# A one-core hybrid block: the second half of q turned by VectorE over DRAM, x1's tiles transposed eight at a time, and another slab order

## The chip, the core and the metric

One core of a Trainium2 chip runs the whole kernel in one launch. The metric is the device time of one execution in microseconds. PE is the matrix engine (TensorE), DVE VectorE, ACT ScalarE, POOL GpSimd, SP the engine whose queue issues most of the DMAs. Each engine runs its own list of instructions in the order in which the program gives them; an instruction that waits holds up all that stand behind it on its engine.

## What is computed

One layer of a trunk with two branches, 512 rows of 1024 columns, float32:

```python
h = rms_norm(x, norm_pre)
(aq, ak, av, az, dq, dk, dv, db, da, dz, gate_att, gate_dn) = split_cols(h @ w_in)
q, k = apply_rope(rms_norm(heads(aq))), apply_rope(rms_norm(heads(ak)))       # 8 and 2 heads of 128
y_att = (gqa_attention(q, k, heads(av)) * silu(az)) @ w_br_att
qkv = silu(short_conv(concatenate([dq, dk, dv])))
o_dn = bidir_gated_deltanet(l2_norm(cq) * 128 ** -0.5, l2_norm(ck), cv, g, beta)   # chunks of 64, both ways
y_dn = (rms_norm(o_dn, dn_norm) * silu(dz)) @ w_br_dn
mix = (sigmoid(gate_att) * y_att + sigmoid(gate_dn) * y_dn) @ w_out
x = x + rms_norm(mix, norm_post)
x = x + rms_norm(sigmoid(x @ w_ple_gate) * (p @ w_ple_proj), ple_norm)
```

The products must hold float32 accuracy, which the kernel reaches by splitting both operands of a gemm into a rounded high half and the rest as a low half, and adding three products: low weight by high data, high by low, high by high.

## The kernel before

**Slabs.** All large weights come in slabs of 128x1024 float32. ACT casts a slab to its high half (`whi`), and POOL (L102) or DVE (L97) subtracts that from the slab to get the low half (`wlo`). A slab with the 512 rows of h takes 24 matmuls of 128x512: L553 to L555 in `gemm_t` for slabs as the stationary operand (dq, dk, dv, az, dz, gA, gB, ydn), L590 to L592 and L572 to L574 where the data is stationary (kv, q0, q1, out0, out1, pg0, pg1). The yatt slabs have their own lines, L1861 for low-by-high and high-by-high, L1845 for high-by-low.

**What sets the order.** The program is laid out by a planner (`Flow`) before anything runs. Its parts are generators; each has a priority, and each step of a part gets an estimated time on its engine. The gemms form one stream of the lowest priority (10), which runs the slab jobs in the order of the table `ORDER`. All other work (convolutions, the chunked recurrence, the heads of attention, the tails of each gemm) are parts with priorities from the table `PR`, and the planner puts their instructions between the matmuls of the stream when it believes their operands ready. So the slab order decides which matmuls PE has at hand while a chain of small steps runs on the other engines. `COOL` and `HOT` are the thresholds by which `split` gives the low half of a slab to POOL or DVE; `EXPS` decides whether an exponential of the recurrence is eight small ACT activations (L983) or one DVE addition (L987) and one large ACT activation; `EOUT` delays a few writes; `VGAP` spaces the steps of the recurrence's preparation.

**The halves of q.** q is computed in two halves of four heads, q0 and q1, each with a tail for every 128 rows (`q_tail`, L1514 on): row norms, rotary turn, then the transpose that the scores need. For a half listed in `QTURN` the tile goes through `small_blocks` (one DVE transpose of 32x32 blocks), is written to a DRAM tensor `Bq` and read back by four DMAs into a tile `c` in the order that completes the transpose (`turned`), and `landed` casts it on ACT and subtracts on POOL or DVE. A half that isn't listed is transposed by four PE matmuls with the identity into a bank `aux` (L1541), and ACT and DVE take the two halves from that bank.

**Attention and its neighbours.** `att_heads` (L1632) runs the scores of a group of four heads: three matmuls (L1657 to L1659) for each head and 128 rows, DVE's maximum of the row, a small scaling on POOL (`sm`), the exponential on ACT, a 32x32 transpose on DVE. Then come the weighted sums, 192 matmuls at L1734, which need each head's tile split into high (ACT) and low (DVE, L97, `blk`). `yatt_two` begins the first two yatt slabs with the half of the rows that the first group of heads gave and finishes them when the second group is done. The inverse of the chunk matrices ends at L1152 and L1167 on PE, with two DVE scalings (64x512) behind, and the recurrence begins at L1222.

**The end.** out0 and out1 give the two halves of x1's row tiles. `out1_tail` normalises and adds; of the four row tiles the first (`TURNED = 1`) goes over DRAM as above, the others are transposed by PE in two groups of four, one for each half, into one `aux` bank each (L1969). pg0 and pg1 follow.

Of the kernel before, what the change touches and what calls it, by code (L numbers as in the profile page):

```python
# [35 lines left out]
class Flow:  # L36
# [87 lines left out]
    def run(self):  # L124
        while self.parts:
# [32 lines left out]


ORDER = """  # L160
dq1 dk2 dk1 dk0 dq3 dk3 dq0 dq2 dv2 az4 dq6 az3 dk5 dv3 dq4 gB6
gA2 dk4 az7 dz1 dz4 dv1 gB5 dz2 az6 dv0 gB0 dq5 dq7 dk6 gB4 dk7
gA0 az0 gB3 dz6 dv6 dv7 gA6 gA5 dv4 dz0 az2 kv dv5 gB2 vec gA7
gB1 az1 dz3 az5 gA3 dz5 q0 dz7 gA1 q1 gA4 gB7 free_h ydn1 ydn2 ydn6
ydn3 ydn0 ydn5 ydn7 ydn4 yatt7 yatt4 yatt6 heads_on0 yatt3 yatt5 yatt0 yatt2 yatt1 heads_on1 out0
out1 pg0 pg1
"""
OUT0 = 'yatt3 yatt1 yatt2 yatt4'
PR = dict(dec=5, dm1=2, y=7, conv=1, gate=6, kv=4, q=9, head=7, ple=9, prep=1, tab=9)
GAP = 0.0  # L170
EXPS = 0.11
SP13 = 480.0
SPARE = ((15, "raw", 7.0, 190.0), (11, "pair", 22.0, 80.0), (12, "pair", 22.0, 80.0), (14, "pair", 279.0, 375.0),
         (13, "pair", 443.0, SP13), (6, "pair", 560.0, 640.0), (14, "raw", 590.0, 640.0))
EOUT = 27.01
WIDE = 2.0
LAND = "c2"
QTURN = (0,)
TURNED = 1
YTURN = ()  # L180
LONG, NEAR = 0.6, 1.5
X_DVE = ()
WARM = 5.5
PVB = 0.695
VGAP = 1.5
HEADHOT = 1
BATCH, TURN = 4, 0.3
SPAREMM = 2
W1 = 0
COOL, HOT = 10.41, -0.29  # L190


@with_exitstack
def layer(ctx, tc, x, xT, pw0, wp1, wt, wba, wn, rows, qkn, hd16, npost, pnorm, dnorm, cs, out):
    nc = tc.nc
    pe, act, dve, pool, sync = nc.tensor, nc.scalar, nc.vector, nc.gpsimd, nc.sync
# [40 lines left out]
    def unit(i, shape, dt=F32):  # L237
        return tile(f"u{i}", shape, dt)

    def bank(tag, shape=(128, 512)):  # L240
        cnt[0] += 1
        return ps.tile(list(shape), F32, tag=tag, bufs=caps[tag], name=f"{tag}_{cnt[0]}")
# [214 lines left out]


    slab, blocks, fetched = {}, {}, {}
    taken, weighed = Event(), Event()  # L460

    lent = {"raw": {}, "pair": {}}
    held = {}
# [1 line left out]
    def lend(u, kind, t0, t1):  # L465

        yield "at", t0
        yield "get", f"u{u}"
        w = unit(u, [128, 2, 1024], F32 if kind == "raw" else F32R)
        tags = [f"{kind}{u}_{i}" for i in range(2 if kind == "raw" else 1)]  # L470
        for i, tag in enumerate(tags):
            F.slots[tag] = [F.now]
            lent[kind][tag] = w[:, i] if kind == "raw" else w
        yield "at", t1
        for tag in tags:
            del lent[kind][tag]
        for tag in tags:
            yield "get", tag
        free(f"u{u}")
# [1152 lines left out]
    def att_heads(g):  # L1632
# [60 lines left out]

        yield "get", "u14"
        ring = unit(14, [128, 2, 2, 16, 32], F32R)
        for i in range(2):
            F.slots[f"ring{i}"] = [F.now]

# [237 lines left out]
    def out1_tail(t, o, need):  # L1936
# [10 lines left out]
        for half, src in enumerate((late["mx0"][:, t, :], o)):  # L1947
# [5 lines left out]
            if t < TURNED:  # L1953
                yield "at", tr - 0.5
                yield "get", "f2"
                T, te = small_blocks(xa[:, hs], tr)
                yield "at", te - 0.5
                yield "get", LAND
                L = tile(LAND, [128, 4, 4, 32])
                tw, te = turned(T, te, f"Bx{t}{half}", L)  # L1960
                free("f2", tw)
                ends.append((L, te))
                continue
            yield "at", tr + 0.3
            yield "get", "aux"
            pt = bank("aux", [128, 4, 128])
            for j in range(4):
                k = half * 4 + j
                pe.transpose(pt[:, j, :], xa[:, k * 128:(k + 1) * 128], ident)  # L1969
            yield "pe", 0.436  # L1970
            cc = slice(t * 128, (t + 1) * 128)
            _, te = split(pt, x1Th[half][:, :, cc], x1Tl[half][:, :, cc], F.now, 512)
            free("aux", te)
        for half, (L, te) in enumerate(ends):
            yield "at", te - 0.5
            te = landed(L, te, x1Th[half], x1Tl[half], t)
        return te + 0.2

    def out_job(half, us):
# [269 lines left out]
```

## Time and profile before

| | |
|---|---|
| three runs | 734.19, 735.26, 736.13 us (median 735.26) |
| the profiled execution | 732.72 us, its span 731.0 us |
| first weight-stationary matmul of the program's own work (L1370) | 5.85 us after the span's start |
| last PE matmul's end | 723.9 us |
| DMA | 121.64 MB, mean 166 GB/s |

The busy figures, the chain, PE's waits and the windows stand in the prediction. To read them: a timeline row is the start in us, the duration in us, the engine, the line, the operation, out<-in by the program's names, the shape, the number of instructions joined in the row, and in brackets the engine's idle time before it with what ended it. Matmuls overlap, so a matmul's duration is longer than the time from its start to the next one's start; the latter is what PE spends on it. Every helper that records an operation has one line (L122 for most, L97 and L102 for the two subtractions), so rows are told apart by names and shapes.

### The profile page before, as it was taken

How to read it: one execution, taken by the hardware profiler on the slowest of the kernel's cores; microseconds unless marked ns; L12 is line 12 of the kernel's file. 1: busy time of each engine (PE TensorE's matmuls, PEld its weight loads, DVE VectorE, ACT ScalarE, POOL GpSimd, SP SyncE). 2: the span in 40 equal slices, each digit the busy share in tenths (PEclk: the TensorE clock that was granted, in tenths of full speed). 3: DMA queues.
4: the chain of work that ended last, by engine and by line, in shares of the span. 5: the costliest groups of instructions: out<-in, count | busy, mean ns of one | idle time of the engine just before them, and what ended most of it. 6: DMA issues, size and time to landing. Idle time of an engine off the chain costs nothing.

```text
span 731.0 us, 12273 instructions
## 1 busy us (share of the span) xinstructions
PE 718.7 (98%) x4577; PEld 601.3 (82%) x4577; DVE 496.2 (68%) x914; ACT 352.6 (48%) x669; POOL 307.4 (42%) x293
## 2 busy tenths in 40 slices
PE   9999999999999999999999999999999999999996
PEld 7688888888789898888888888888888778888885
DVE  4688979889785667896946443658979974314534
ACT  6658653753651365435442236345746554323522
POOL 5836495111421265114411145655344638163501
PEclk9999999999999999999999999999999999999999
DMA  9854529856421324767350234695468568337313
GB/s 355 301 175 133 195 87 282 265 173 230 103 96 37 101 101 113 234 202 201 121 158 15 87 115 142 198 226 155 163 196 207 192 220 309 135 95 256 110 57 117
DMA packets 79051, 121.64 MB, mean 166 GB/s; under 512 B 24400, under 2 KB 42768, under 8 KB 78992
## 3 DMA queue, kind: packets, MB, share of 16 engines
q1 hardware_dynamic: 78848, 120.73, 52.4%
q8 instruction: 36, 0.59, 0.3%
q14 instruction: 23, 0.19, 0.1%
q10 hardware_dynamic: 144, 0.13, 0.1%
HBM read 94.98 MB, written 25.85 MB: 165 GB/s over the span
## 4 chain that ended last, share of the span: by engine, by line
PE 85%; DVE 8%; ACT 3%; issue 2%; DMA 1%; POOL 1%; POOLq 0%; SPq 0%; DVEq 0%; ACTq 0%
PE mm L553 15%; PE mm L555 14%; PE mm L554 14%; PE mm L574 4%; PE mm L572 4%; PE mm L573 4%; PE mm L592 3%; PE mm L590 3%; PE mm L591 3%; DVE f L122 3%; PE aux L1222 2%; PE aux L1254 2%; PE aux L1240 2%; PE aux L1213 1%; PE aux L1202 1%
## 5 line engine op out<-in xcount | busy, mean ns | idle before, releaser
L553 PE MATMUL mm<-u,wlo 128*128 128x512 f32 x488 | 195.9, 402 | 0.4 <-DVE wlo L97 0.4
L555 PE MATMUL mm<-u,whi 128*128 128x512 f32 x488 | 190.4, 390 | 0.0
L554 PE MATMUL mm<-u,whi 128*128 128x512 f32 x488 | 190.2, 390 | 0.0
L102 POOL TENSOR_TENSOR wlo<-wraw,whi 128x1024 fp32r<-128x1024 f32 x47 | 113.0, 2406 | 178.4 <-ACT whi L122 146.9
L553 PEld LDWEIGHTS mm<-u,wlo 128*128 128x128 f32 x488 | 91.8, 188 | 19.7 <-ACT u L122 0.8
L555 PEld LDWEIGHTS mm<-u,whi 128*128 128x128 f32 x488 | 91.6, 188 | 19.7
L554 PEld LDWEIGHTS mm<-u,whi 128*128 128x128 f32 x488 | 91.8, 188 | 17.0
L122 ACT CAST whi<-wraw 128x1024 fp32r<-128x1024 f32 x61 | 63.9, 1047 | 57.6 <-PE mm L555 20.1
L122 DVE SCALAR_TENSOR_TENSOR f<-mm,cw,f 128x510 f32<-128x510 f32 (+1 forms) x96 | 71.4, 746 | 9.0 <-ACT f L122 6.6
L102 POOL TENSOR_TENSOR u<-wraw,u 128x1024 fp32r<-128x1024 f32 x18 | 43.1, 2403 | 27.6 <-ACT u L122 26.0
L572 PE MATMUL mm<-u,u 128*128 128x512 f32 (+1 forms) x136 | 51.8, 381 | 0.0
L574 PE MATMUL mm<-u,u 128*128 128x512 f32 (+1 forms) x136 | 51.3, 377 | 0.0
L573 PE MATMUL mm<-u,u 128*128 128x512 f32 (+1 forms) x136 | 51.2, 377 | 0.0
L122 DVE TENSOR_TENSOR u<-aux,u 128x512 f32<-128x512 f32 (+2 forms) x49 | 31.6, 664 | 12.9 <-PE aux L1043 6.4
L122 ACT COPY c<-aux 128x512 f32<-128x512 f32 x18 | 10.4, 585 | 48.2 <-DVE f L122 35.4
L590 PE MATMUL mm<-whi,u 128*128 128x512 f32 x80 | 31.4, 393 | 0.0
L122 ACT ACTIVATE mm<-f 128x512 f32<-128x512 f32 x24 | 14.4, 600 | 35.0 <-DVE f L122 35.0
L592 PE MATMUL mm<-whi,u 128*128 128x512 f32 x80 | 31.2, 390 | 0.0
L591 PE MATMUL mm<-wlo,u 128*128 128x512 f32 x80 | 31.1, 389 | 0.0
L102 POOL TENSOR_TENSOR u<-u,u 128x1024 fp32r<-128x1024 f32 (+1 forms) x11 | 22.0, 2004 | 20.9 <-ACT u L122 15.6
L574 PEld LDWEIGHTS mm<-u,u 128*128 128x128 f32 x136 | 25.6, 188 | 4.8
L573 PEld LDWEIGHTS mm<-u,u 128*128 128x128 f32 x136 | 25.6, 188 | 4.6
(297 smaller groups left out, 1504.2 us busy)
## 6 DMA issues: line engine op xcount, KB each, us to landing
wraw<-in_wt_dram SPq DMA_DIRECT2D x58, 512.0 KB, 3.6
wraw<-in_wn_dram SPq DMA_DIRECT2D x24, 512.0 KB, 4.1
u<-in_wt_dram SPq DMA_DIRECT2D x14, 512.0 KB, 6.3
u<-CI SPq DMA_DIRECT2D x16, 256.0 KB, 5.5
u<-VD SPq DMA_DIRECT2D x16, 256.0 KB, 6.7
u<-in_x_dram SPq DMA_DIRECT2D x4, 512.0 KB, 7.6
u<-in_xT_dram SPq DMA_DIRECT2D x4, 512.0 KB, 8.2
eD<-u SPq DMA_DIRECT2D x8, 256.0 KB, 9.0
```

Of the source, the lines that this page charges most:

```text
L102: ins = fn(*a, **k)
L122: fn(*a, **k)
L553: pe.matmul(o, lo[:, k, :], mh(k), start=(k == 0), stop=False)
L554: pe.matmul(o, hi[:, k, :], ml(k), start=False, stop=False)
L555: pe.matmul(o, hi[:, k, :], mh(k), start=False, stop=(k == 7))
L572: pe.matmul(o, b, hi, start=(i == 0), stop=False)
L573: pe.matmul(o, a, lo, start=False, stop=False)
L574: pe.matmul(o, a, hi, start=False, stop=(i == 7))
L590: pe.matmul(o[t], b, hi, start=(k == 0), stop=False)
L591: pe.matmul(o[t], a, lo, start=False, stop=False)
L592: pe.matmul(o[t], a, hi, start=False, stop=(k == 7))
L1222: pe.matmul(pw[:, h, :], Vm[g][d][:, 4 * c + h, :], r[:, h, :], start=True, stop=True)
```

## The change

`ORDER` and `OUT0` are new permutations of the same slabs; PR, EXPS, EOUT, VGAP, COOL and HOT get other values; QTURN lists both halves of q; `out1_tail` takes two banks and transposes both halves of a tile in one run; and `lend` of unit 14, which lends its space to a slab, now waits for an event that `att_heads` sets once the ring of the second group has that unit.

```diff
-OUT0 = 'yatt3 yatt1 yatt2 yatt4'
-PR = dict(dec=5, dm1=2, y=7, conv=1, gate=6, kv=4, q=9, head=7, ple=9, prep=1, tab=9)
+OUT0 = 'yatt5 yatt1 yatt7 yatt0'
+PR = dict(dec=0, dm1=11, y=5, conv=1, gate=4, kv=2, q=7, head=8, ple=3, prep=7, tab=9)
-EXPS = 0.11
+EXPS = 0.94
-EOUT = 27.01
+EOUT = 37.16
-QTURN = (0,)
+QTURN = (0,1)
-VGAP = 1.5
+VGAP = 1.2
-COOL, HOT = 10.41, -0.29
+COOL, HOT = 8.39, -3.14
...
+        if u == 14 and t0 > 500.0:
+            yield "ev", ringed
...
         ring = unit(14, [128, 2, 2, 16, 32], F32R)
+        if g == 1:
+            ringed.set(F.now)
...
-            yield "at", tr + 0.3
+        for half, (L, te) in enumerate(ends):
+            yield "at", te - 0.5
+            te = landed(L, te, x1Th[half], x1Tl[half], t)
+        if t < TURNED:
+            return te + 0.2
+        yield "at", tr + 0.3
+        pts = []
+        for half in range(2):
             yield "get", "aux"
-            pt = bank("aux", [128, 4, 128])
+            pts.append(bank("aux", [128, 4, 128]))
+        for half, pt in enumerate(pts):
             for j in range(4):
                 k = half * 4 + j
                 pe.transpose(pt[:, j, :], xa[:, k * 128:(k + 1) * 128], ident)
-            yield "pe", 0.436
-            cc = slice(t * 128, (t + 1) * 128)
+        yield "pe", 0.872
+        cc = slice(t * 128, (t + 1) * 128)
+        for half, pt in enumerate(pts):
             _, te = split(pt, x1Th[half][:, :, cc], x1Tl[half][:, :, cc], F.now, 512)
             free("aux", te)
```

Of the table of slabs only the part around attention is shown, first the two lines before and then the two after:

```diff
-gB1 az1 dz3 az5 gA3 dz5 q0 dz7 gA1 q1 gA4 gB7 free_h ydn1 ydn2 ydn6
-ydn3 ydn0 ydn5 ydn7 ydn4 yatt7 yatt4 yatt6 heads_on0 yatt3 yatt5 yatt0 yatt2 yatt1 heads_on1 out0
+gA5 gA7 gA1 gB7 dz2 q0 az5 dz5 q1 gB5 gB4 free_h ydn0 ydn3 ydn7 ydn4
+ydn6 ydn5 ydn2 heads_on1 ydn1 yatt6 yatt0 yatt2 yatt7 yatt5 yatt1 yatt4 yatt3 heads_on0 vec out0
```

The program's order on the engines follows from this, with the line numbers of the later places moved by 2 to 9 (L553 is L555 after, L1657 is L1659, L1734 is L1738, L1861 is L1865). The first place is on PE, before the change, at the end of the q1 stage: the third group of q1's transposes, the end of the slab gB7 (`mm_4948`) and the first scores.

```order
L555 MATMUL mm_4948<-u_14_137,whi_4848 128x512
L1541 MATMUL aux_4997<-ident,f_661_4915 128x128 x4
L553 MATMUL mm_4948<-u_14_137,wlo_4849 128x512
L554 MATMUL mm_4948<-u_14_137,whi_4848 128x512
L555 MATMUL mm_4948<-u_14_137,whi_4848 128x512
L1657 MATMUL mm_5013<-u_417_3249,u_580_4394 128x512
```

After the change PE passes there from the last slab of h (gB4, `mm_4972`) to the scores with no transpose between.

```order
L555 MATMUL mm_4972<-u_14_137,wlo_4907 128x512
L556 MATMUL mm_4972<-u_14_137,whi_4906 128x512
L557 MATMUL mm_4972<-u_14_137,whi_4906 128x512
L1659 MATMUL mm_5030<-u_410_3232,u_576_4406 128x512
L1660 MATMUL mm_5030<-u_410_3232,u_575_4405 128x512
```

All four L1541 rows (of four transposes each) are gone; what they wrote now comes through the tiles `c` below. The second place is on POOL, in the score stage of the first group of heads, before the change: the small scalings `sm` of the softmax and low halves of slabs, and behind them the products with the gate.

```order
L102 TENSOR_TENSOR wlo_5009<-wraw_4901,whi_5008 128x1024
L122 TENSOR_SCALAR sm<-sm,saq 128x1 x11
L102 TENSOR_TENSOR wlo_5141<-wraw_5022,whi_5140 128x1024
L122 TENSOR_SCALAR sm<-sm,saq 128x1 x5
L102 TENSOR_TENSOR wlo_5232<-wraw_5058,whi_5231 128x1024
L102 TENSOR_TENSOR u_716_5264<-u_716_5264,gi_5359 128x512
```

After the change the same stretch of POOL, where the tiles `c` are those that the reads of Bq fill for q1:

```order
L122 TENSOR_SCALAR sm<-sm,saq 128x1 x5
L102 TENSOR_TENSOR u_621_4702<-c_669_5014,u_620_4701 128x4x128
L122 TENSOR_SCALAR sm<-sm,saq 128x1 x3
L102 TENSOR_TENSOR u_621_4702<-c_672_5024,u_620_4701 128x4x128
L122 TENSOR_SCALAR sm<-sm,saq 128x1
L102 TENSOR_TENSOR wlo_5153<-wraw_5037,whi_5152 128x1024
L122 TENSOR_SCALAR sm<-sm,saq 128x1 x3
L102 TENSOR_TENSOR u_621_4702<-c_679_5038,u_620_4701 128x4x128
L102 TENSOR_TENSOR wlo_5232<-wraw_5080,whi_5231 128x1024
L122 TENSOR_SCALAR sm<-sm,saq 128x1 x4
```

Three of q1's four subtractions have moved in between the scalings (the fourth is on DVE), each behind its cast on ACT. The third place is on PE, from the last score to the first weighted sums of the second group, before the change; the rows left out are those of ydn7 (`mm_5804`), ydn4 (`mm_5872`) and the first yatt slab (`mm_5928`).

```order
L1659 MATMUL aux_5811<-u_417_3249,u_625_4692 128x512
L553 MATMUL mm_5804<-u_354_2801,wlo_5680 128x512
...
L555 MATMUL mm_5872<-u_575_4389,whi_5801 128x512
L1861 MATMUL mm_5928<-u_753_5590,wlo_5864 128x512
L1861 MATMUL mm_5928<-u_753_5590,whi_5863 128x512
...
L1845 MATMUL mm_5928<-u_754_5591,whi_5863 128x512 x4
L1734 MATMUL aux_5857<-blk_5887,u_752_5589 128x512
```

After the change, with three matmuls of ydn2 (`mm_5797`), ydn1 (`mm_5922`) and the first yatt slab (`mm_5972`):

```order
L1661 MATMUL mm_5880<-u_410_3232,u_620_4701 128x512
L555 MATMUL mm_5797<-u_571_4401,wlo_5673 128x512
...
L555 MATMUL mm_5922<-u_350_2820,wlo_5772 128x512
L557 MATMUL mm_5922<-u_571_4401,whi_5771 128x512
L1865 MATMUL mm_5972<-u_754_5652,wlo_5893 128x512
L1865 MATMUL mm_5972<-u_754_5652,whi_5892 128x512
...
L1738 MATMUL aux_5911<-blk_5916,u_753_5651 128x512
```

Between the last score and the first yatt matmul stand 45 rows before and 27 after; 12 yatt matmuls stand ahead of the weighted sums before and 6 after, and the six others have moved behind the sums. The last score, of three matmuls, now stands directly behind two others of its head.

More of the change, by code (lines that the diff above doesn't have):

```diff
@@ L160 @@
 ORDER = """
-dq1 dk2 dk1 dk0 dq3 dk3 dq0 dq2 dv2 az4 dq6 az3 dk5 dv3 dq4 gB6
-gA2 dk4 az7 dz1 dz4 dv1 gB5 dz2 az6 dv0 gB0 dq5 dq7 dk6 gB4 dk7
-gA0 az0 gB3 dz6 dv6 dv7 gA6 gA5 dv4 dz0 az2 kv dv5 gB2 vec gA7
-gB1 az1 dz3 az5 gA3 dz5 q0 dz7 gA1 q1 gA4 gB7 free_h ydn1 ydn2 ydn6
-ydn3 ydn0 ydn5 ydn7 ydn4 yatt7 yatt4 yatt6 heads_on0 yatt3 yatt5 yatt0 yatt2 yatt1 heads_on1 out0
+dq0 dk2 dk1 dk3 dq1 dk0 dq3 dq2 dv2 dz4 dk5 az4 dq4 dv3 dq7 dz6
+gB0 dk4 dz3 gB1 az1 dv1 az3 gA0 gA4 dv0 az6 dq6 dk7 az2 dz1 dq5
+dk6 gB3 gB6 gA2 dv7 gA6 dv4 dz7 gA3 gB2 kv dv6 az0 dv5 dz0 az7
+gA5 gA7 gA1 gB7 dz2 q0 az5 dz5 q1 gB5 gB4 free_h ydn0 ydn3 ydn7 ydn4
+ydn6 ydn5 ydn2 heads_on1 ydn1 yatt6 yatt0 yatt2 yatt7 yatt5 yatt1 yatt4 yatt3 heads_on0 vec out0
 out1 pg0 pg1
 """
-OUT0 = 'yatt3 yatt1 yatt2 yatt4'
-PR = dict(dec=5, dm1=2, y=7, conv=1, gate=6, kv=4, q=9, head=7, ple=9, prep=1, tab=9)
+OUT0 = 'yatt5 yatt1 yatt7 yatt0'
+PR = dict(dec=0, dm1=11, y=5, conv=1, gate=4, kv=2, q=7, head=8, ple=3, prep=7, tab=9)
 GAP = 0.0
-EXPS = 0.11
+EXPS = 0.94
 SP13 = 480.0
@@ L459, in layer @@
     slab, blocks, fetched = {}, {}, {}
-    taken, weighed = Event(), Event()
+    taken, weighed, ringed = Event(), Event(), Event()
     lent = {"raw": {}, "pair": {}}
@@ L1962, in out1_tail @@
                 ends.append((L, te))
-                continue
-            yield "at", tr + 0.3
+        for half, (L, te) in enumerate(ends):
[6 more added lines that the diff above has]
+        for half in range(2):
             yield "get", "aux"
-            pt = bank("aux", [128, 4, 128])
+            pts.append(bank("aux", [128, 4, 128]))
+        for half, pt in enumerate(pts):
             for j in range(4):
@@ L1969, in out1_tail @@
                 pe.transpose(pt[:, j, :], xa[:, k * 128:(k + 1) * 128], ident)
-            yield "pe", 0.436
-            cc = slice(t * 128, (t + 1) * 128)
+        yield "pe", 0.872
+        cc = slice(t * 128, (t + 1) * 128)
+        for half, pt in enumerate(pts):
             _, te = split(pt, x1Th[half][:, :, cc], x1Tl[half][:, :, cc], F.now, 512)
             free("aux", te)
-        for half, (L, te) in enumerate(ends):
-            yield "at", te - 0.5
-            te = landed(L, te, x1Th[half], x1Tl[half], t)
         return te + 0.2
```

## The prediction

> **What bounds the kernel now.** I read the page's busy line and its chain first.
>
> ```profile
> PE 718.7 (98%) x4577; PEld 601.3 (82%) x4577; DVE 496.2 (68%) x914; ACT 352.6 (48%) x669; POOL 307.4 (42%) x293
> PEclk9999999999999999999999999999999999999999
> PE 85%; DVE 8%; ACT 3%; issue 2%; DMA 1%; POOL 1%; POOLq 0%; SPq 0%; DVEq 0%; ACTq 0%
> ```
>
> PE is busy 98% of the span, at nine tenths or more of its clock in every slice, and carries 85% of the chain that ended last. So the time is PE's work plus the few places where it stands still. Those places are listed by the waits of PE.
>
> ```profile
> PE mm L2110 <- POOL ident masks.py:199: 1.4, 1, 1.4
> PE mm L1861 <- DVE u L97: 0.7, 1, 0.7
> PE aux L1132 <- issue: 0.7, 1, 0.7
> PE mm L1861 <- POOL wlo L102: 0.6, 1, 0.6
> PE mm L675 <- POOL u L102: 0.4, 1, 0.4
> PE mm L553 <- DVE wlo L97: 0.4, 1, 0.4
> PE mm L881 <- DVE partk L122: 0.3, 1, 0.3
> PE aux L1486 <- DVE f L97: 0.3, 1, 0.3
> PE mm L1370 <- DVE u L97: 0.2, 1, 0.2
> ```
>
> Behind the first row, which belongs to the start, only eight waits stand, 3.6 us in all. A new order can gain no more than that by better hiding; everything else must come from work taken off PE. It can lose far more, since every one of the slab jobs needs its low half in time. The engine nearest to PE is DVE, and the windows show where it is fullest.
>
> ```profile
> 500.00:520.00 20.00, 20.00 (x90) 16.48 (x90) 17.36 (x31) 11.68 (x28) 8.41 (x16) 1.00 0.30 93
> 520.00:540.00 20.00, 20.00 (x207) 16.49 (x206) 18.39 (x31) 14.03 (x27) 6.32 (x5) 1.00 0.64 213
> 560.00:580.00 20.00, 19.35 (x84) 15.34 (x83) 17.98 (x30) 12.65 (x27) 10.22 (x12) 1.00 0.78 253
> 580.00:600.00 20.00, 19.30 (x227) 15.61 (x226) 15.93 (x22) 11.75 (x17) 6.63 (x4) 1.00 0.46 165
> ```
>
> After the length the columns are PE, PEld, DVE, ACT, POOL. Through the scores and the first weighted sums of attention (500 to 540) PE has no gap although DVE is busy 17.4 and 18.4 of 20 us; at 560 to 600 PE loses 0.65 and 0.70. This is the stage into which the change puts new DVE and POOL work.
>
> **The change part by part.**
>
> *Transposes of q1.* The four groups of L1541 go. What one costs PE is seen between its neighbours:
>
> ```profile
> 494.79 0.39 PE L555 MATMUL mm<-u,whi 128*128 128x512 f32 x1
> 495.02 0.60 PE L1541 MATMUL aux<-ident,f 128*128 128x128 f32 x4
> 495.37 0.47 PE L553 MATMUL mm<-u,wlo 128*128 128x512 f32 x1
> 495.69 0.39 PE L554 MATMUL mm<-u,whi 128*128 128x512 f32 x1
> 495.91 0.39 PE L555 MATMUL mm<-u,whi 128*128 128x512 f32 x1
> ```
>
> A 128x512 matmul follows its predecessor by 0.23 us. From the group's start to the next matmul are 0.35, and that one holds the next for 0.32, 0.09 more than usual: 0.44 for a group, four groups **-1.77 us**. All of it is PE time in a stage without PE gaps, so it is gained unless PE waits for it later. [...]
>
> In its place, per tile: one DVE block transpose, one write and four reads over DRAM, an ACT cast and a POOL or DVE subtraction instead of the same pair from the bank.
>
> ```profile
> L1541 PE MATMUL aux<-ident,f 128*128 128x128 f32 x16 | 2.4, 272 | 0.0
> L122 DVE STREAM_TRANSPOSE f<-f 128x512 f32<-128x512 f32 x12 | 8.3, 702 | 0.1
> L102 POOL TENSOR_TENSOR u<-c,u 128x512 fp32r<-128x512 f32 x4 | 5.2, 1292 | 0.0
> L97 DVE TENSOR_TENSOR u<-c,u 128x512 fp32r<-128x512 f32 x6 | 4.4, 734 | 10.8 <-ACT u L122 10.7
>   ACT u L122: 7.8, 4
> ```
>
> DVE pays 4 x 0.70 and is spared three subtractions of about 0.73, since the order puts three of the four on POOL at 1.29: +0.6 us on DVE, +3.9 on POOL, both off PE's path as long as the scores keep their distance. The last row is from the view of the tile Bq, the waits that it caused, here of half q0: its four casts on ACT waited 7.8 us together for the reads, nearly 2 us each. Behind such a cast on ACT now stand softmax exponentials and slab casts, and behind the POOL subtraction the small scalings that the exponentials need. Half q0 paid this in a stage of plain gemms and PE did not feel it. On SP the 20 new DMAs stand between slab loads. I cost it at nothing: the cover is the rows of slab matmuls between the scores. If it is gone, PE waits for the held operation, 3 x 1.29 = 3.9 us by the POOL row, or 3 x (1.29 + 1.95) = 9.7 with the wait for the reads. Below nothing it can't go, as no PE work is hidden behind it.
>
> *x1 in runs of eight.* The same 24 transposes remain; two groups of four, 0.44 each, stand together instead of apart. The 0.09 that a following matmul loses could be paid once instead of twice: three tiles, -0.3 at best; against it the second bank and a later start of the first half, at worst one subtraction (0.73) at the last tile. I take 0, which lies nearer to the small gain.
>
> *New slab order before attention.* The chain's milestones keep their places to within 18 matmuls (4.1 us). Two shift towards a wait. The sums that waited for partk (L881, 0.3 above) come six matmuls later, 1.4 us of cover: **-0.3**. The last step of the triangular inverse stood 18 matmuls ahead of the recurrence that needs it, and now six:
>
> ```profile
> 203.13 0.71 DVE L122 STREAM_TRANSPOSE f<-u 128x512 f32<-128x512 f32 x1
> 206.82 2.08 PE L1167 MATMUL aux<-u,blk 64*64 64x64 f32 x64
> 208.84 0.50 PE L553 MATMUL mm<-u,wlo 128*128 128x512 f32 x1
> 212.44 0.67 DVE L122 TENSOR_SCALAR u<-aux 64x512 f32<-64x512 f32 x1
> 213.07 1.16 PE L1222 MATMUL aux<-u,u 128*128 128x128 f32 x9
> ```
>
> Six matmuls behind 208.84 end at 210.2. DVE's queue from 203.13 to this scaling loses a set of convolution products there and has 5.8 us left (this transpose, one reduction and six operations of some 0.7 to 0.77), so its two scalings end near 210.3: **+0.1**, with 0 and +0.8 (one DVE operation more) as bounds. ACT exponentials for DVE sums (EXPS), the POOL threshold (COOL, HOT), later eD writes and the norm vectors' later load move work between engines that are 42 to 68% busy: 0. Of the other waits in the list (L1132, L675, L553, L1486, together 1.8) I assume that the new order has as many; none of them hangs on a rule that changed, so each may go or be doubled, -1.8 to +1.8.
>
> *The way into the first yatt.* Here rows of the trace decide.
>
> ```profile
> L102 POOL TENSOR_TENSOR wlo<-wraw,whi 128x1024 fp32r<-128x1024 f32 x47 | 113.0, 2406 | 178.4 <-ACT whi L122 146.9
> ...
> 565.88 0.39 PE L1659 MATMUL aux<-u,u 128*128 128x512 f32 x1
> 570.38 0.65 DVE L122 TENSOR_REDUCE sm<-aux 128x1 f32<-128x512 f32 x1
> 571.13 0.26 POOL L122 TENSOR_SCALAR sm<-sm,saq 128x1 f32<-128x1 f32 x1
> ...
> 574.31 4.23 DVE L97 TENSOR_TENSOR blk<-u,blk 128x512 fp32r<-128x512 f32 x3 [0.38 <-ACT blk L122]
> 574.54 2.85 POOL L102 TENSOR_TENSOR wlo<-wraw,whi 128x1024 fp32r<-128x1024 f32 x1
> ...
> 577.45 0.50 PE L1861 MATMUL mm<-u,wlo 128*128 128x512 f32 x1 [0.60 <-POOL wlo L102]
> ...
> 589.90 2.36 DVE L97 TENSOR_TENSOR u<-wraw,u 128x1024 fp32r<-128x1024 f32 x2 [1.11 <-ACT u L122]
> 592.32 2.11 PE L1861 MATMUL mm<-u,u 128*128 128x512 f32 x8 [0.69 <-DVE u L97]
> ```
>
> Before, 45 matmuls lie between the last score and the first of yatt, which waits 0.6 for its low half on POOL. After it are 27, so PE arrives 27 x 0.23 + 0.23 = 6.4 us behind the last score. On POOL this low half is queued behind the last scaling of the softmax. If that ends where it did, 571.39 - 565.88 = 5.5, and the subtraction takes 2.4 (the mean of the first row), the half is ready at 7.9: a wait of 1.5, 0.9 more. In exchange six matmuls of the first pair now stand behind the weighted sums, where PE waited 0.7 for the second pair's low half at 592.32; 1.4 us of cover take that wait away. Sum **+0.2**; bounds -1.3 (neither wait is left) and +2.1: two block transposes more in DVE's queue ahead of the last maximum (1.4), and a subtraction of 2.85 (0.45 more). That 2.85 stands beside DVE subtractions that took 4.23 for three instead of 2.2. [...]
>
> Sum: -1.77 + 0 - 0.3 + 0.1 + 0.2 = **-1.8 us**. The profiled execution took 732.7 us and would take 730.9; the three runs have their median at 735.26, 2.5 above it, so I forecast 735.26 - 1.8 = **733.5**.
>
> **The rivals.**
> 1. *Slower: POOL's queue holds the softmax.* The new subtractions wait for their DRAM reads with the score scalings behind them, PE runs out of slab rows between the scores, and the wait before yatt grows to its bound. For it: the 7.8 us of ACT's waiting, DVE at 17 to 18 of 20 us. Against it: POOL is at 8.4 and 6.3 of 20, and no score waited before. Price 3.9 + 1.9 more: 733.5 + 5.8 = 739.3; it decides once a score's scaling comes later than the matmuls that stand between two scores. Half of it gives 736.4. Chance 0.17.
> 2. *The gain is waited away.* The attention stage is paced by DVE, so PE arrives 1.77 us earlier at the first yatt and waits that much longer there. For it: DVE's load, and that the half's POOL queue hangs on DVE's last maximum. Against it: the scores themselves start earlier by the same time, and PE had no gap there. 735.26 - 1.8 + 1.77 = 735.2. Chance 0.24.
> 3. *The order is also better hidden.* The four waits assumed unchanged (1.8) and the 1.5 before yatt go for the most part: 733.5 - 2.5 = 731.0. For it: a 27-row cover is enough if the maximum comes sooner, as three scores now stand in a row; against it: nothing in the rows shows why. Chance 0.20. A full 0.272 us for each removed transpose (2.6 more, 730.9) would look alike: 0.03.
> 4. The change not doing what it says: the order shows the L1541 rows gone, so none.
>
> **How the numbers follow.** The forecast has 0.36. A measurement tells 0.3% (2.2 us) from no change: faster is below 733.05, slower above 737.47. The forecast, with its 1 us of unknown waits, lies a third below: 0.13; rival 3 and its neighbour nearly all, 0.22; rival 2 a little, 0.03: faster 0.38. Slower is two thirds of rival 1 and a rest: 0.14. Same 0.48. For 8 in 10 the range takes in rivals 2, 3 and the smaller half of rival 1: 730.3 to 737.3.
>
> **What would show it.** No L1541 rows and PE busy time about 1.8 us lower; DMA waits of ACT casts for Bq doubled without waits of score rows; one wait of 1 to 2 us at the first row of yatt (L1861, numbered L1865 after) for POOL's low half, none at the second pair; L881 without its wait. Waits at score rows, or PE windows under 20.0 between 500 and 540, would make rival 1; a PE busy time lower by 1.8 with the waits before yatt higher by as much, rival 2.

## The result and the profile after

The changed kernel takes 744.79 us (three runs, 743.86 to 746.3) against 735.26 (734.19 to 736.13), 9.5 us more. The ratio on record is 1.0148, 95% interval 1.0129 to 1.0166; the quotient of these two medians is 1.0130, at the lower end of it. In the sets of the experiments the kernel before took 733.5 to 733.8, so the loss is known as 9.5 to 11 us. The forecast was 733.5, and the range ended at 737.3. Of run 13 below, one execution of 3866 us is left out. The profiled execution of after is the one of 744.79 us, with a span of 742.8, against 731.0: 11.8 more.

The busy line and the clock of the page of after:

```profile
PE 720.9 (97%) x4561; PEld 602.3 (81%) x4561; DVE 489.3 (66%) x907; ACT 361.6 (49%) x709; POOL 316.0 (43%) x297
PEclk9999999999999999999999999999999999999998
```

PE has 16 matmuls less (4577 to 4561, the transposes of q1) and is yet busy for 2.2 us longer; DVE is busy for 6.9 less. So no engine became the bound. PE's waits behind the start grow from 3.6 to 12.8 us, and these 9.2 with the 2.2 of busy time are nearly all of the 11.8. The waits of PE in after (total us, times, longest):

```profile
PE mm L555 <- DVE wlo L97: 3.1, 3, 2.0
PE mm L1865 <- POOL wlo L102: 2.8, 1, 2.8
PE aux L1659 <- ACT c L122: 2.7, 1, 2.7
PE mm L2119 <- POOL ident masks.py:199: 1.4, 1, 1.4
PE mm L555 <- issue: 1.1, 1, 1.1
PE mm L555 <- DVE u L122: 0.9, 1, 0.9
...
PE mm L883 <- DVE partk L122: 0.4, 1, 0.4
```

Five rows are new or several times their size: three at slabs of h (L555, for DVE's low half, for an issue, for a tile `u`), one at a score (L1659), one at the first yatt row (L1865). The windows say where (length, then PE, PEld, DVE, ACT, POOL, the granted clock, the DMA share, GB/s):

```profile
140.00:160.00 20.00, 19.19 (x85) 15.55 (x85) 16.51 (x30) 12.47 (x34) 0.89 (x1) 1.00 0.90 289
160.00:180.00 20.00, 18.01 (x80) 14.60 (x79) 17.09 (x36) 13.07 (x37) 1.86 (x3) 1.00 0.45 149
520.00:540.00 20.00, 20.00 (x101) 16.32 (x103) 18.31 (x33) 14.13 (x28) 10.83 (x12) 1.00 0.65 202
540.00:560.00 20.00, 17.27 (x204) 13.54 (x201) 10.08 (x17) 7.82 (x13) 6.63 (x6) 0.95 0.64 183
580.00:600.00 20.00, 17.24 (x183) 14.44 (x185) 17.17 (x29) 13.33 (x25) 8.86 (x9) 0.91 0.34 103
```

Two stages lose. Long before attention, at 140 to 180, PE has gaps of 0.8 and 2.0 us, where the trace of before has none (20.00 and 20.00); gaps of 1.1 and 0.9 follow at 360.7 and 492.1. In attention the second group's scores and the way to its weighted sums lose 2.7 and 2.8, and the granted clock falls to 0.95 and 0.91. Where the scores of the first group stand (520 to 540), PE is full as before.

Put into stages by the starts of the first score and of the weighted sums, with the slab matmuls that the trace shows between them:

| | before | after | difference |
|---|---|---|---|
| first score | 498.7 | 503.1 | +4.4 us |
| first score to first weighted sum, group 0 | 31.2 | 36.0 | +4.8 us |
| its slab matmuls, between the scores and behind the last | 42 + 45 | 54 + 54 | +21 |
| first score to first weighted sum, group 1 | 36.2 | 38.7 | +2.5 us |
| its slab matmuls, between the scores and behind the last | 48 + 57 | 51 + 33 | -21 |
| end of PE's last matmul | 723.9 | 735.5 | +11.6 us |

The slab matmuls of this stage are a fixed stock (in both orders 1680 stand ahead of the first score). Six more have moved from between the two groups to behind the second sums; they make the one stretch 1.4 us shorter and the other 1.3 longer, which cancels. After the change the plan spends 21 more of them in group 0, which at 0.227 us is the whole of the +4.8; no wait shows there. Group 1 then has 21 less, should be 4.8 shorter, and is 2.5 longer: 7.3 us are lost in it.

This is the score wait of group 1 in the timeline of after (start, duration, engine, line, operation, shape, idle before):

```profile
554.60 0.39 PE L557 MATMUL mm<-u,whi 128*128 128x512 f32 x1
555.26 1.26 POOL L102 TENSOR_TENSOR u<-u,gi 128x512 f32<-128x512 f32 x1 [2.24 <-DMA gi<-SR]
556.50 0.27 POOL L122 TENSOR_SCALAR sm<-sm,saq 128x1 f32<-128x1 f32 x1
556.80 0.78 ACT L122 ACTIVATE c<-aux,sm,saq 128x512 f32<-128x512 f32 x1 [10.67 <-POOL sm L122]
557.72 0.56 PE L1659 MATMUL aux<-u,u 128*128 128x512 f32 x1 [2.73 <-ACT c L122]
558.93 0.63 PE L555 MATMUL mm<-u,wlo 128*128 128x512 f32 x1
559.36 0.63 PE L556 MATMUL mm<-u,whi 128*128 128x512 f32 x1
...
561.47 0.39 PE L1659 MATMUL aux<-u,u 128*128 128x512 f32 x1
```

Read upwards from PE: the score waits for a bank that an exponential on ACT frees; that waits for its scaling `sm` on POOL; and that stands behind a product with the gate (`u<-u,gi`), which sat 2.24 us for its DMA read. It is rival 1's picture, with the gate's product in the place of q1's subtractions. And behind the wait the matmuls follow each other by 0.43 us in place of 0.23, until 561.47: nine in 3.75 us. The casts that wait for q1's reads are not in this chain; over the whole trace such casts waited 6.6 us in six, against 7.8 in four before.

The other wait, on the way into yatt, in the same view:

```profile
578.97 0.39 PE L1661 MATMUL mm<-u,u 128*128 128x512 f32 x1
580.40 1.29 POOL L102 TENSOR_TENSOR u<-u,gi 128x512 f32<-128x512 f32 x1 [1.66 <-issue]
581.97 0.78 ACT L122 ACTIVATE u<-aux,sm,saq 128x512 f32<-128x512 f32 x1 [2.33 <-POOL sm L122]
582.87 1.47 DVE L122 STREAM_TRANSPOSE u<-u 128x512 f32<-128x512 f32 x2 [2.18 <-ACT u L122]
584.27 1.25 DVE L122 TENSOR_REDUCE sm<-mm 128x1 f32<-128x512 f32 x2
585.61 0.27 POOL L122 TENSOR_SCALAR sm<-sm,saq 128x1 f32<-128x1 f32 x1 [0.33 <-DVE sm L122]
585.84 2.35 POOL L102 TENSOR_TENSOR wlo<-wraw,whi 128x1024 fp32r<-128x1024 f32 x1
588.24 0.50 PE L1865 MATMUL mm<-u,wlo 128*128 128x512 f32 x1 [2.76 <-POOL wlo L102]
```

The last score is issued at 578.97. DVE's last two maxima are queued behind two block transposes that wait for exponentials, and those for a scaling behind a gate product. The last scaling ends at 585.88, 6.9 us behind the score (5.5 before), and the low half of the yatt slab at 588.19.

### The profile page after: what moved, and what is told of

Its sections match the earlier page's. It is cut to its first block, busy times and chain, and to the rows that moved or that the text cites. A ratio compares the mean times of both kernels' runs of the same rounds, so it can differ in the third digit from the quotient of the medians.

```text
span 742.8 us, 12346 instructions
## 1 busy us (share of the span) xinstructions
PE 720.9 (97%) x4561; PEld 602.3 (81%) x4561; DVE 489.3 (66%) x907; ACT 361.6 (49%) x709; POOL 316.0 (43%) x297
## 5 line engine op out<-in xcount | busy, mean ns | idle before, releaser
L555 PE MATMUL mm<-u,wlo 128*128 128x512 f32 x488 | 196.0, 402 | 5.1 <-DVE wlo L97 3.1
L102 POOL TENSOR_TENSOR wlo<-wraw,whi 128x1024 fp32r<-128x1024 f32 x50 | 119.8, 2396 | 161.7 <-ACT whi L122 120.9
L555 PEld LDWEIGHTS mm<-u,wlo 128*128 128x128 f32 x488 | 92.0, 189 | 25.3 <-DVE wlo L97 3.6
L102 POOL TENSOR_TENSOR u<-wraw,u 128x1024 fp32r<-128x1024 f32 x16 | 38.2, 2401 | 13.3 <-ACT u L122 13.3
L122 DVE TENSOR_TENSOR u<-aux,u 128x512 f32<-128x512 f32 (+2 forms) x45 | 28.8, 662 | 9.9 <-PE aux L1045 6.3
L102 POOL TENSOR_TENSOR u<-u,u 128x1024 fp32r<-128x1024 f32 (+1 forms) x12 | 24.3, 2042 | 22.0 <-ACT u L122 16.6
L122 ACT ACTIVATE go<-mm 128x512 f32<-128x512 f32 x32 | 18.9, 591 | 25.7 <-PE mm L557 25.7
L594 PE MATMUL mm<-whi,u 128*128 128x512 f32 x80 | 31.2, 390 | 0.0
L102 POOL TENSOR_SCALAR_AFFINE_SELECT u<-u 128x512 f32<-128x512 f32 x16 | 11.7, 748 | 43.7 <-DVE blk L1076 16.5
```

The lines of the kernel that those rows point to most:

```text
L102: ins = fn(*a, **k)
L122: fn(*a, **k)
L555: pe.matmul(o, lo[:, k, :], mh(k), start=(k == 0), stop=False)
L594: pe.matmul(o[t], a, hi, start=False, stop=(k == 7))
```

## The experiments

The expectations speak of four theories. **A**: POOL's queue, with the gate's products ahead of the scalings, sets attention's time. **B**: the landing of q1 does (reads of Bq on SP, casts on ACT, subtractions). **C**: the exponentials that EXPS moved to ACT hold the casts of slabs in the early stages. **D**: cover, the slab matmuls that PE has left while a chain runs on the other engines. Times are medians with their range; ratios are to the kernel before on the same chip (733.47 to 733.83 in these sets).

**1. The scalings off POOL's queue.** After, with one engine changed:

```diff
-te = G(0.2, te, pool.tensor_scalar, out=bi, in0=mx, scalar1=rs, ...
+te = G(0.2, te, dve.tensor_scalar, out=bi, in0=mx, scalar1=rs, ...
```

> The changed kernel with the softmax's small scalings (sm) issued on DVE instead of POOL; the plan and every other instruction keep their place. Theory A (POOL's queue: a gate product that waits for its read of SR stands ahead of the scalings, so the scores and the low half of the first yatt slab come late): the waits of PE at the score row and at the first L1865 row, 2.7 and 2.8 us in the changed kernel, fall below 1 us each, the matmuls behind them run at 0.23 us instead of 0.43, and the time falls from 744.8 by 6 to 9 us, to 736 to 739. Theory B (q1's way over DRAM makes the softmax late): both waits stay, 744.8 within 1.5. DVE gets 32 operations of some 0.1 to 0.2 us, which could cost up to 1 us under either.

745.29 us (744.66 to 746.0), 1.0161 [1.0146, 1.0176]: as slow as after. The wait at 557.7 is gone and that at yatt is 1.1 instead of 2.8, but waits of 0.3 to 1.0 us appear at seven other places of attention. The scaling takes 204 ns on DVE, 6.5 us for all 32, so DVE's load has grown too, and the run alone doesn't refute theory A; yet one of the two largest waits in attention was dissolved and the other more than halved without any gain.

**2. Exponentials back to DVE.** After, with `A(1.94, t, exps)` replaced by a DVE addition and one ACT exponential at the same place.

> The changed kernel with each set of eight small exponentials on ACT replaced, at the same place of the plan, by one DVE addition and one large ACT exponential. Theory C (the sets, 2.0 us each on ACT and more of them since EXPS was raised, stand ahead of slab casts, and that gives the waits of 0.8 and 2.0 us at L555 near 145 and 170 us): both waits fall below 0.4 us in sum, time 744.8 - 2.5 to 3.3 = 741.5 to 742.3, the two waits in attention unchanged. Rival (DVE's own load of those stretches gives these waits, 16.5 and 17.1 of 20 us): the DVE additions make them longer, 745 to 748.

749.9 (747.67 to 752.68), 1.0225 [1.0197, 1.0253]. The early waits grew (L883 for DVE's partk 2.4, L555 for DVE's low halves 4.5 together). Theory C falls in this form: DVE, which the windows of after show busy for 16.51 and 17.09 of 20 us there, took the work only with longer waits.

**3. q1 turned by PE again.** After, with `QTURN = (0,)`.

> The changed kernel with QTURN = (0,): q1 transposed on PE again, the order replanned behind it. Theory A: gate products still stand among the scalings, the waits in attention stay, and the 1.8 us of transposes come back: 745 to 748. Theory B: the waits in attention go, 744.8 - 9 + 1.8 = 737 to 738.

739.87 (739.36 to 743.4), 1.0103 [1.0074, 1.0131]. The windows of attention in it:

```profile
540.00:560.00 20.00, 20.00 (x192) 16.43 (x185) 15.15 (x27) 9.84 (x19) 13.68 (x10) 1.00 0.57 138
560.00:580.00 20.00, 18.72 (x82) 14.77 (x81) 17.41 (x32) 14.23 (x32) 11.61 (x18) 1.00 0.73 229
580.00:600.00 20.00, 20.00 (x231) 16.56 (x232) 18.88 (x26) 12.40 (x19) 3.22 (x2) 1.00 0.44 155
```

Both long waits are gone, the clock stays at 1.00 here, and the slab matmuls are 39 + 45 and 48 + 54, nearly those of before. So q1 over DRAM costs 3 to 5 us in the new order (3.3 by the two ratios, 4.9 by the medians 744.79 and 739.87, neither better known than to some 2.5 us), although it spares PE 1.8. The rest of the slowdown is there without it, and all of it ahead of attention: in this trace the first score comes at 505.2, against 498.7 before, and PE ends at 730.6, against 723.9.

**4. q1 over DRAM in the old order.** Before, with `QTURN = (0,1)`.

> The kernel before with QTURN = (0, 1) alone, replanned. Theory A: here only two gate products stand ahead of a scaling, with one scaling and one score behind them, so 735.3 - 1.8 = 733.5, up to 736 if those two cost a wait at yatt. Theory B: q1's landings make the softmax late here too, 740 or more.

745.85 (745.2 to 746.79), 1.0169 [1.0154, 1.0184]. Its waits begin:

```profile
PE aux L1734 <- ACT blk L122: 8.0, 1, 8.0
PE aux L1657 <- ACT u L122: 3.0, 2, 2.7
```

The plan puts off the first weighted sums until q1's last tile has landed (`att_heads` waits for that event), 111 slab matmuls now run ahead of them instead of 45, and none is left behind the last score of group 1: PE stands still for 8.0 us at its sums. The time is within what theory B forecast too (740 or more); what speaks for D are the counts.

**5. q1 one slab earlier in the new order.** After, `q0 az5 dz5 q1` turned into `q0 az5 q1 dz5`.

> The changed kernel with q1's gemm one slab earlier (q1 ahead of dz5), so that its tiles land before the scores need the tile slots. By its order 60 slab matmuls stand behind the last score ahead of the second weighted sums, as against 33 in the changed kernel and 57 before. Theory D (cover: the slab matmuls are a fixed stock of about 200 for the whole attention stage; q1's way over DRAM makes the plan spend more of them ahead of the first weighted sums, and PE then has too few behind the last score): the two waits of 2.8 us and the slow matmuls behind them go, 9 us at most, so 744.8 to 735.5 - 739. Theory A (gate products ahead of scalings on POOL): three gate products still stand among the scalings, so at least one of the two waits stays at 2 us or more, 741 to 745.

752.86 (750.18 to 753.58), 1.0248 [1.0226, 1.0271]. Group 1 has 60 matmuls behind its last score and no wait, as theory D says, but its forecast of 735.5 to 739 misses by 14: waits of 3.9 (L555 for a tile of DVE) and 6.2 (L1659 for ACT) stand in group 0. Eight reads of Bq in a row took 3.96 us of SP's queue, and ACT's cast of a landed tile waited 4.18. The cost has moved, not gone.

**6. The same in the old order.** Before, `QTURN = (0,1)` and `dz7 gA1 q1` turned into `dz7 q1 gA1`.

> The kernel before with QTURN = (0, 1) and q1's gemm one slab earlier (q1 ahead of gA1), nothing else. By its order 51 slab matmuls stand behind the last score, where QTURN alone left none. Theory D: the 8.1 and 2.8 us waits of that run vanish and what is left is the prediction's first term, 733.7 - 1.8 = 731.9 (731 to 733.5). Theory B (the landings themselves hold POOL, ACT and SP): waits in the scores stay, 738 or more.

739.05 (737.76 to 739.38), 1.007 [1.0057, 1.0083]. Attention is as short as before (31.0 and 36.2 us), as theory D says, yet its forecast of 731.9 misses by 7. The loss stands ahead of the first score, which comes at 503.7 instead of 498.7: new waits of 1.5 and 1.1 at q1's own gemm (L590, for tiles that DVE frees), and one of 0.8 at L553; the mean granted clock of its profiled execution is 0.995, against 0.997 and 0.998 in the runs of before beside it. Whether q1 so close behind q0 would wait there with its transposes on PE was not run.

**7. Only the cover moved.** Before, nothing added: the planner's clock for the first weighted sums is moved by 5.4 us, so that slab rows pass ahead of them.

```diff
+        if g == 0:
+            yield "at", F.now + 5.4
```

> The kernel before, q1 on PE, with one edit: the plan lets the first weighted sums begin 5.4 us later than it would, so that 66 instead of 45 slab matmuls go ahead of them and 24 instead of 57 are left behind the last score. No work is added. Theory D: PE waits about (57 - 24) x 0.227 = 7.5 us behind the last score, with a slow clock after it, and the time is 740 to 743. Theories A and B: q1 and the order of the gate products are as before, so 733.7 within 1.5.

740.54 (739.84 to 741.08), 1.0092 [1.0078, 1.0106]. The weighted sums of group 1 in its timeline:

```profile
585.04 0.79 PE L1736 MATMUL aux<-blk,u 32*128 32x512 f32 x3 [4.71 <-ACT blk L122]
...
586.36 0.63 PE L1736 MATMUL aux<-blk,u 32*128 32x512 f32 x3
```

33 slab matmuls fewer stand behind the last score of group 1, PE waits 4.71 us there and issues at a slow spacing behind it: the sums come 0.42 us apart at 588.48 and 588.90 and 0.24 at 589.63, and the granted clock over 580 to 600 is 0.83. If all of that loss stands at a clock of 0.50, it lasts 6.8 us by estimate (0.17 x 20 / 0.50). The work is that of before to the last instruction, no new operation is in any queue, and 7 us are lost. The first score comes 0.8 us later than in the trace of before; the rest of the loss stands behind the last score. This is theory D by itself.

**8. EXPS alone put back.** After, `EXPS = 0.11`.

> The changed kernel with EXPS = 0.11 as before, replanned; its order in the attention stage is that of the changed kernel. If the raised EXPS gives the waits near 145 and 170 us (a set of small exponentials ahead of a slab cast on ACT), they go: 744.8 - 3.3 = 741.5. If the new slab order gives them, they stay: 744.8 within 1. The attention waits stay under either.

743.8 (739.9 to 748.8), 1.0141 [1.01, 1.0181]. The early waits stay in its trace (L555 for DVE's low halves 3.1 in all), which speaks against theory C again. The times scatter by 9 us, the traced execution is the slowest of the four, and by the times alone no difference to after can be told, nor the 741.5 excluded.

**9 to 11. The other parts of the change alone, on the kernel before.** First ORDER and OUT0.

> The kernel before with the new ORDER and OUT0 alone (old PR, EXPS, EOUT, VGAP, COOL and HOT; q1 and x1 as before). If the slab order gives the changed kernel's waits ahead of attention (near 145, 170, 360 and 492 us, 6 us with their followers), they are here too: 733.5 + 5 = 737 to 740, and none in attention, as its order leaves 59 slab matmuls behind the last score (theory D). If the new numbers give them, the time is 733.5 within 1.5.

Then PR, EXPS, EOUT, VGAP, COOL and HOT.

> The kernel before with the new PR, EXPS, EOUT, VGAP, COOL and HOT alone (old slab order; q1 and x1 as before). If these numbers give the waits ahead of attention: 737 to 740; if the slab order does: 733.5 within 1.5. In attention its order leaves 48 slab matmuls behind the last score (theory D: no wait over 1 us), but has gate products among the scalings on POOL (theory A: a wait of 2 us or more).

Then `out1_tail` in runs of eight.

> The kernel before with the new out1_tail alone: x1's later tiles transposed in one run of eight. The prediction took 0 (-0.3 to +0.7): 733.5, 733.2 to 734.2. Rival: the later start of the first half's two subtractions delays pg0's first matmuls, a wait at L572 and 734.5 or more.

The order: 739.05 (737.67 to 740.98), 1.0074 [1.0057, 1.0091]. The numbers: 749.69, 1.0218 [1.0204, 1.0232]. x1: 733.63, 1.0002 [0.9994, 1.0011]. The order alone brings the wait near 169. Its rows in the timeline of run 9:

```profile
165.10 2.02 ACT L983 ACTIVATE u<-u,cj 128x64 f32<-128x64 f32 x8
167.01 1.04 ACT L122 CAST whi<-wraw 128x1024 fp32r<-128x1024 f32 x1
169.36 0.50 PE L553 MATMUL mm<-u,wlo 128*128 128x512 f32 x1 [2.14 <-DVE wlo L97]
```

The same place of after:

```profile
165.35 2.01 ACT L985 ACTIVATE u<-u,cj 128x64 f32<-128x64 f32 x8
167.26 1.03 ACT L122 CAST whi<-wraw 128x1024 fp32r<-128x1024 f32 x1
168.32 1.23 DVE L97 TENSOR_TENSOR wlo<-wraw,whi 128x1024 fp32r<-128x1024 f32 x1 [0.84 <-ACT whi L122]
169.60 0.50 PE L555 MATMUL mm<-u,wlo 128*128 128x512 f32 x1 [1.99 <-DVE wlo L97]
```

And the same place of before:

```profile
161.62 2.01 ACT L983 ACTIVATE u<-u,cj 128x64 f32<-128x64 f32 x8
163.54 1.03 ACT L122 CAST whi<-wraw 128x1024 fp32r<-128x1024 f32 x1
164.60 1.23 DVE L97 TENSOR_TENSOR wlo<-wraw,whi 128x1024 fp32r<-128x1024 f32 x1 [0.83 <-ACT whi L122]
165.88 0.50 PE L553 MATMUL mm<-u,wlo 128*128 128x512 f32 x1
```

The slab's cast stands behind a set of exponentials on ACT, DVE waits for the cast, PE for DVE; POOL, which could have made the low half, is busy for 1.86 of the 20 us. The queue was the same before, and PE didn't wait, but without any reserve: the low half was ready at 165.83 and PE took it at 165.88. After the change the set of exponentials comes 3.7 us later and PE only 1.7, so PE stands for the 2.0 between. The wait at 145.6 can't be put down to the order: run 11, whose matmuls are those of before up to 671 us, has one of 1.1 there.

The numbers alone cost 16 us on the old order, and their trace has the loss ahead of attention (first score at 513.7; with 48 slab matmuls behind the last score no wait of attention is over 1.3 us). With the new order, and without q1 over DRAM, they add hardly anything to the 5.5 of the order (739.87 in run 3, which has both, against 739.05). The costs of the parts don't add: 12.2 (q1, run 4), 5.5 and 16.2 us alone, 9.5 together.

**12 and 15. q1 over DRAM, other places in the old order.** Before with `QTURN = (0,1)`; run 12 has q0 ahead of dz5 and q1 ahead of gA1, run 15 also q's priority at 6 and the landing of q1 planned 3 us later.

> The kernel before with QTURN = (0, 1), q0 ahead of dz5 and q1 ahead of gA1, so that two slabs stand between the two gemms of q as before, and three behind q1. By its order 51 slab matmuls stand behind the last score. Theory D with q1's gemm free of the waits for banks that q1 close behind q0 gave (1.7, 1.2 and 0.9 us): 733.5 - 1.8 = 731.7, 731 to 733. Theory B (the read of Bq takes longer than planned and holds ACT, DVE or POOL wherever it falls): waits of 1 us or more in the scores, 735 or more.

> The kernel before with QTURN = (0, 1), q0 ahead of dz5 and q1 ahead of gA1, PR q = 6, and q1's landing planned 3 us later (near what the reads took). By its order the casts stand behind the reads with room, and 60 slab matmuls stand behind the last score. Theories B and D together: no wait over 1 us in attention, 733.5 - 1.8 = 731.7, up to 734 with small waits. If a third cause is in it: 738 or more.

741.76 (739.84 to 742.39), 1.0112 [1.0097, 1.0128], and 744.88 (743.12 to 746.01), 1.0143 [1.0124, 1.0163]. In run 12's timeline the landing itself holds a score:

```profile
507.86 5.52 SPq L122 DMA_DIRECT2D c<-Bq  x4
...
516.82 0.62 ACT L122 CAST u<-c 128x512 fp32r<-128x512 f32 x1 [3.30 <-DMA c<-Bq]
517.34 0.77 ACT L122 ACTIVATE u<-mm,sm,saq 128x512 f32<-128x512 f32 x1
...
519.78 0.50 PE L1657 MATMUL aux<-u,u 128*128 128x512 f32 x1 [2.50 <-ACT u L122]
```

The cast sits 3.30 us at the head of ACT's queue, with exponentials behind it. So theory B holds for this wait, as the prediction's rival 1 had it, with ACT in the place of POOL. It is 2.5 of some 8 us; the first score, too, comes 3.4 us later than before (502.0). Planning the landing later (run 15) spread the waits (1.1 to 2.3 at five places) and gained nothing, though 60 slab matmuls stand behind the last score. The forecast of 731.7, the same for both, misses by 10 and 13.

**13 and 16. Work where PE waits.** After, with twelve 128x512 matmuls, whose result is thrown away, ahead of the first yatt row.

```diff
+                if half == 0 and n == n1:
+                    for _ in range(12):
+                        pe.matmul(o[n][0], hi[:, 0, :], ya[0][0][:, 0, :], start=True, stop=True)
```

> The changed kernel with twelve more 128x512 matmuls ahead of the first yatt matmul (on the high half and data that are already there, into a bank that the first real matmul clears), 12 x 0.227 = 2.7 us of added PE work in the place where PE waited 2.8 us; no other instruction moves. Theory D (PE lacks work there, and the slow matmuls behind the wait are the clock's answer to the idle time): the added work is free, the matmuls behind it run at 0.23 us instead of 0.43, and the time is 0.5 to 1.5 us lower than the changed kernel's, 743.3 to 744.3. Rival (the wait is not idle PE time, or the slow matmuls come from something else): 744.8 + 2.7 = 747.5.

> The kernel after with twelve matmuls of 128x512 more (2.7 us at 0.227 each), whose result is thrown away, ahead of the first yatt matmul, where PE waited 2.76 us and then issued at 0.427 us apiece for some 3.5 us. Theory D with the clock (a wait of over some 2.5 us costs again as much as 1.5 us behind it): the wait at 588 falls under 0.5 us, the matmuls behind it come 0.227 apart, the first weighted sums start within 0.3 us of where they did or up to 1.5 earlier, and the time is 743.3 to 744.8. The score wait at 557.7 and its slow matmuls stay as they are. Theory that the slow spacing belongs to the sums' own data or banks and not to the wait: the matmuls of the first weighted sums stay 0.42 apart without a wait ahead of them, 744.8. Theory that nothing was waited for there (the time is set by PE's work alone): 2.7 us more, 747.5.

744.91 us (742.91 to 745.67), 1.0139 [1.0118, 1.0161], and 745.08 (744.29 to 745.51), 1.0149 [1.0129, 1.0168]. Twelve matmuls, 2.7 us, cost nothing. The timeline of run 16:

```profile
556.77 0.39 PE L557 MATMUL mm<-u,whi 128*128 128x512 f32 x1
559.05 0.50 PE L1659 MATMUL aux<-u,u 128*128 128x512 f32 x1 [1.89 <-ACT c L122]
...
585.66 2.88 PE L1865 MATMUL mm<-u,whi 128*128 128x512 f32 x12
588.38 0.47 PE L1868 MATMUL mm<-u,wlo 128*128 128x512 f32 x1
588.70 0.39 PE L1868 MATMUL mm<-u,whi 128*128 128x512 f32 x1
588.92 0.39 PE L1868 MATMUL mm<-u,wlo 128*128 128x512 f32 x1
```

The added twelve fill the wait, and behind the first of the real ones the matmuls come 0.22 to 0.24 apart instead of 0.43: the slow spacing belongs to the wait and not to these matmuls. Up to 585 the program is that of after, and there the same score waits 1.89 instead of 2.73, with no slow matmul behind it. Group 1 takes 35.8 us to its sums, 2.9 less than in the trace of after, but this execution's first score came 2.2 later (505.2). The gain of 0.5 to 1.5 us that the returned clock was expected to bring does not show in the time, so what the slow matmuls cost the whole kernel is not shown. Single traces of one program differ by some 2 us in where they wait, and the stages above are known no better than that.

**14. Gate products believed late.** After, with the planner's time for the gate's product moved by 3 us (`t += 3.0`), so that it is queued behind more scalings.

> The changed kernel with the gate product planned 3 us later, so that most gate products stand behind the scalings (two of eight are left among the first group's successors, one among the second's last); its order leaves 28 slab matmuls behind the last score, fewer than the 33 of the changed kernel. Theory A (POOL's queue sets the waits): 737 to 740. Theory D (too few slab matmuls behind the last score, whatever holds the chain): no better than the changed kernel, 743 to 747.

744.84 (743.06 to 746.24), 1.0137 [1.0113, 1.0161]. The wait at 557.7 is gone, 28 slab matmuls are left behind the last score, and waits of 1.6 and 1.8 us stand at a late score and at the sums. The 737 to 740 of theory A did not come, and it is refuted as what sets the time: it names who is last, and when that one is moved another is last at the same cost.

## Why the prediction was wrong

**Transposes of q1, -1.77.** The rows are gone. Their size was not measured apart; what replaced them outweighed them at every place tried.

**q1's way over DRAM, 0.** This step failed: "I cost it at nothing: the cover is the rows of slab matmuls between the scores." It is worth +3 to +5 in the new order (run 3), and on the old one +12.2, +5.6, +8.2 and +11.1 (runs 4, 6, 12, 15 by medians). The rows were indeed between the scores, and in group 0 nobody waited. But they were taken from the same stock that covers group 1, and the prediction checked the cover only at the stretch next to its edit. Its third place in the program's order showed the loss (45 rows to 27 ahead of yatt), and the text priced it as a wait of 1.5 us at one row. That moving rows alone costs 7 us is shown by run 7; that q1 over DRAM moves them in the changed kernel, by the counts of run 3 against after. No run gave the rows back to group 1 with q1 over DRAM and nothing else changed (run 5 tried, and lost more elsewhere), so that the rows are the whole of the 3 to 5 is argued and not shown. Runs 6, 12 and 15 also move q in the order, and that move alone was not run.

**The way into the first yatt, +0.2.** The mechanism was right, place and engine too: one wait for POOL's low half behind the last scaling, and none left at the second pair (0.6 in the trace of run 16). Mis-sized was the last scaling's end, taken as "5.5" behind the last score and measured at 6.9, since DVE's last maxima wait behind transposes; the half is ready 9.2 behind the score instead of 7.9, the wait 2.76 instead of 1.5. The slow matmuls behind it (0.43 instead of 0.23 apart) were in no term.

**Other waits, assumed unchanged, -1.8 to +1.8.** This step failed as well. The four waits themselves hardly changed (0.6, 0.4, 0.3, and the one at L1486 gone). But the bounds were taken from the waits that the old order has, and a new order makes waits where there were none: at 169.6, 360.7 and 492.1 us PE stands for 2.0, 1.1 and 0.9, besides 0.8 at 145.6, and the first score comes 4.4 later in spite of the transposes saved. Run 9 shows the three, at 169.4, 362.4 and 493.5, with the order alone, and +5.5 us. That milestones keep their distance in matmuls was the wrong view: what counts is when each slab's low half is ready on ACT's and DVE's queues against the moment at which PE asks for it, and before the change that reserve was 0.05 us at one slab that no list of waits names. Only this one of the three was followed to its rows. The L881 wait, forecast to go (-0.3), stayed at 0.4; at the recurrence (+0.1) PE did not wait.

**EXPS, COOL, HOT and the rest, 0 because engines are "42 to 68% busy".** Wrong as a reason: on the old order they cost 16 us (run 10). With the new order they cost nearly nothing, so the sum was not hurt, by luck.

**x1 in eights, 0.** Right (run 11).

**The rivals.** Rival 1 had the right kind, but its price of 5.8 counted held operations one by one. Of its signs, a wait at a score row showed and the wait before yatt grew to 2.76; windows under 20.0 between 500 and 540 did not show, since the loss came one group later. Its place is seen in after's rows and yet doesn't set the time (runs 1 and 14). Rivals 2 and 3 both end no higher than the kernel before, and nothing of them is seen.

Of the slowdown, then, some 6 us belong to order and numbers together (run 3: 739.87 against 733.7) and the rest, 3 to 5, to q1 over DRAM. Left open is why q1 over DRAM is costly even where group 1 keeps its cover (runs 5, 6, 12 and 15, in all of which theory D's forecast was too low): each such run shows other waits, at SP's reads, ACT's casts or DVE's tiles, and no single one was isolated. No kernel here beats before.

## What to carry to other kernels

Where a plan puts filler work between the steps of a chain, count the filler as a stock over the whole stage: rows that an added step consumes early are missing at the next chain, and the wait appears there, under another engine's name (8.0 us in run 4 and 4.71 in run 7, both put down to ACT). The engine that a wait names can be the last of several near each other: in runs 1 and 14 the wait of 2.73 us at 557.7 went and the time stayed, at 745.29 and 744.84. So before mending it, move it and see whether the time follows. A new order is costed by the time at which each consumer's operand will be ready, with the reserve it had in the old order, not by the waits that the old order happened to have.

## What the runs showed of the hardware

A wait of PE can cost more than itself: behind some waits the granted clock is 0.50, and 128x512 matmuls come 0.427 us apart instead of 0.227. In after:

```profile
554.62:558.03 3.41, 0.68 (x3) 1.00 1.00 181
558.03:561.45 3.42, 3.42 (x9) 0.50 0.38 106
```

The rows give a stretch's length, PE's busy time, the granted clock, the DMA share and GB/s. The second stretch at 0.50 in after, from 588.75 to 592.17 behind the wait of 2.76 us, is as long, 3.42 us, and begins 30.72 us behind the first. In run 5, behind a wait of 3.90 us, the spacing of 0.43 lasts longer, from 513.29 to 517.98 at least.

The length of a wait alone does not decide, and the 2.5 us of run 16's expectation are no limit. Behind 2.44 us (run 2, at 85.47) the matmuls come 0.43 apart; behind 2.69 (run 4, at 572.63), 2.50 (run 12), 2.31 (run 15, at 582.85), 2.14 (run 9), 1.99 (after, at 169.60) and 1.89 (run 16, at 559.05) they come 0.22 to 0.24 apart from the second on. Behind 2.47 us in run 2 (at 593.13) the third to the fifth matmul come 0.23 to 0.24 apart, and the spacing is 0.36 at 594.54 and 0.42 to 0.43 from 595.69 on. What decides besides the length is not shown.

SP's queue can be held by a short row of DMAs: four reads of Bq took 5.52 us in run 12, from the start of the first to the end of the last, where one read takes 0.42 at the median in after and four in a row, from 524.04 on, took 1.74. What held the four in run 12 is not shown. The queue's next DMA, `SR<-rrow`, came behind them, at 513.94.
